# Trace of a batched matrix product: A's columns for five rows of B, transposed by VectorE in 32x32 blocks and copied from quadrant to quadrant, in place of TensorE transposes

## The chip, the cores and the metric

The kernel runs on one core of one Trainium2 chip. A core has a matrix engine (TensorE, PE in the profile), a vector engine (VectorE, DVE), a scalar engine (ScalarE, ACT), GpSimd (POOL) and a synchronisation engine (SyncE, SP), one on-chip memory of 128 partitions (SBUF), an accumulator memory (PSUM), and 16 DMA engines. The metric is the device time of one execution in microseconds (us); less is better.

## The reference

```python
def setup_inputs():
    B, N = 8, 2176
    return {"a": np.random.randn(B, N, N).astype(np.float32),
            "b": np.random.randn(B, N, N).astype(np.float32)}

def reference(a, b):
    prod = np.matmul(a, b)
    traces = np.diagonal(prod, axis1=1, axis2=2).sum(axis=-1)
    return traces.astype(np.float32)
```

Only the diagonal of each product is summed, so each of the eight results is the sum over i and j of a[i, j] * b[j, i]: every element of A and of B is used once, A transposed against B. A and B are read once each, 2 x 8 x 2176 x 2176 x 4 bytes, 303 MB.

## The kernel before, in words

A matrix is 17 blocks of 128 rows ("rows" below always means such blocks of 128). `load` brings rows from DRAM to SBUF through `fetch`, a DMA issued by POOL that casts float32 to bf16 on the way. `fetch` issues every load in one fixed order: `in_order` ties each issue to the one before. In a group of m rows, partition p holds the m consecutive matrix rows m*p to m*p + m - 1, so that each partition reads one long run of DRAM.

For a batch the loads are A's first five rows (into pool `middle`, one buffer), A's other twelve (`stage`, two buffers of twelve rows; two groups of six in one DMA), then B's five (`middle` again) and B's twelve (`stage`). The lists are `a_loads = b_loads = [(1, 5), (2, 6)]`. Batch 0 starts with one row of A that SP loads as float32 and ScalarE and VectorE cast (`load_first`), then four, then twelve; the last batch loads A's twelve before its five, and B in small pieces.

`transpose_group` turns one group of A's rows into the tile `at` ([128, 17, 2176] bf16, one buffer), whose layout matches B's. Because B's groups interleave rows too (`even = [5, 6, 6]`), the columns of A that belong to one of B's rows lie bm apart, with bm the rows of B's group. For B's groups of an even number of rows, pairs of neighbouring bf16 columns are read as one float32 word and transposed together by TensorE (L151); for the group of five, `singles`, they are transposed one at a time as bf16 (L175). The results go to PSUM tiles `ps` (three buffers of pool `psum`, tag `aT`), and `evacuate` copies them into `at`: every fourth copy by VectorE (L121), the others by ScalarE (L123).

When A's 17 rows of a batch stand in `at`, `on_dve` issues `multiply_reduce` on VectorE (L128) for B's five rows and then for B's twelve: each multiplies `at` by the rows of B, writes the product over `at` and sums it into one column of `sums`. `tc.issue_after` puts these behind the batch's last VectorE copy. The last batch gives part of B to TensorE (L287), and its B groups are `fine = [4, 4, 4, 2, 1, 1, 1]`, which have no group of five.

The waits around the change: POOL's load of B's five rows needs `middle` free, so it waits for the last transpose that reads A's five rows. POOL's load of the next batch's five rows of A needs `middle` free again, so it waits for the multiply-reduce of B's five rows, which in turn needs the whole of `at`, so all copies of A's twelve rows. Behind it in POOL's order stands the load of the next batch's twelve rows. The next batch's copies into `at` wait for the multiply-reduces that read it. Tile, the framework, places the waits; each engine runs its instructions in order.

Of the kernel before, what the change touches and what calls it, by code (L numbers as in the profile page):

```python
# [20 lines left out]
def kernel(  # L21
# [6 lines left out]
    nc = tc.nc  # L28
    P = 128
    BATCH, N, N2 = a.shape  # L30
    assert N == N2 and N % P == 0
    NT = N // P
    MOST, MID = 12, 5

    bf16 = mybir.dt.bfloat16
    f32 = mybir.dt.float32
# [21 lines left out]
    at_pool = ctx.enter_context(tc.tile_pool(name="at_pool", bufs=1))  # L58
    stage = ctx.enter_context(tc.tile_pool(name="stage", bufs=2))
    middle = ctx.enter_context(tc.tile_pool(name="middle", bufs=1))  # L60
    single = ctx.enter_context(tc.tile_pool(name="single", bufs=1))
    psum_pool = ctx.enter_context(tc.tile_pool(name="psum", bufs=3, space=bass.MemoryType.PSUM))
    psum_small = ctx.enter_context(tc.tile_pool(name="psum_small", bufs=1, space=bass.MemoryType.PSUM))

# [22 lines left out]
    def load_first(src, start):  # L87

        words = stage.tile([P, MOST, N], bf16, tag="stage")
        plain = words.bitcast(f32).rearrange("p r k -> p (r k)")[:, :N]  # L90
        half = N // 2
        t = single.tile([P, 1, N], bf16, tag="single")
        nc.sync.dma_start(out=plain, in_=src[start:start + P, :])
        nc.scalar.copy(out=t[:, 0, :half], in_=plain[:, :half])  # L94
        nc.vector.tensor_copy(out=t[:, 0, half:], in_=plain[:, half:])  # L95
        return t
# [18 lines left out]
    evacs = 0  # L115
    last_copy = None

    def evacuate(dst, src):
        nonlocal evacs, last_copy
        if evacs % 4 == 3:  # L120
            last_copy = nc.vector.tensor_copy(out=dst, in_=src)  # L121
        else:
            nc.scalar.copy(out=dst, in_=src)  # L123
        evacs += 1

    def multiply_reduce(x, y, acc, out=None):

        nc.vector.tensor_tensor_reduce(  # L128
            out=x if out is None else out, in0=x, in1=y, scale=1.0, scalar=0.0,
            op0=MUL, op1=ADD, accum_out=acc,  # L130
        )

    def transpose_group(at, a_t, start, m, b_groups):

        words = a_t.bitcast(f32)
        dst = at[:, :, start:start + P * m].rearrange("q v (p r) -> q v p r", r=m)
        pairs, singles = [], []
        for b_start, bm in b_groups:
            v = b_start // P
            if bm % 2 == 0:  # L140
                for t in range(bm // 2):
                    pairs.append((v + 2 * t, b_start // 2 + t, bm // 2))
            else:
                singles += [(v + r, b_start + r, bm) for r in range(bm)]

        for at0 in range(0, len(pairs), 8 // m):
            some = pairs[at0:at0 + 8 // m]
            ps = psum_pool.tile([P, 8, P], f32, tag="aT")
            for n, (v, c0, step) in enumerate(some):
                for r in range(m):  # L150
                    nc.tensor.transpose(  # L151
                        ps[:, n * m + r, :],
                        words[:, r, c0:c0 + step * (P - 1) + 1:step],
                        tiles[f32],
                    )
            if m == 1:
                v0 = some[0][0]
                evacuate(
                    dst[:, v0:v0 + 2 * len(some), :, 0].rearrange("q (n s) p -> q n s p", s=2),
                    ps.bitcast(bf16).rearrange("q n (p s) -> q n s p", s=2)[:, 0:len(some), :, :],  # L160
                )
                continue
            for n, (v, _, _) in enumerate(some):
                evacuate(
                    dst[:, v:v + 2, :, :],
                    ps[:, n * m:(n + 1) * m, :].bitcast(bf16).rearrange("q r (p s) -> q s p r", s=2),
                )
        for at0 in range(0, len(singles), 16 // m):
            some = singles[at0:at0 + 16 // m]
            ps = psum_pool.tile([P, 8, P], f32, tag="aT")  # L170
            ps16 = ps.bitcast(bf16).rearrange("q a b -> q (a b)")[:, 0:len(some) * m * P]
            ps16 = ps16.rearrange("q (n r p) -> q n r p", r=m, p=P)
            for n, (v, c0, step) in enumerate(some):
                for r in range(m):
                    last_transpose = nc.tensor.transpose(  # L175
                        ps16[:, n, r, :],
                        a_t[:, r, c0:c0 + step * (P - 1) + 1:step],
                        tiles[bf16],
                    )
            v0 = some[0][0]  # L180
            evacuate(dst[:, v0:v0 + len(some), :, :], ps16.rearrange("q n r p -> q n p r"))
        return last_transpose

    pe_work = []
# [13 lines left out]
    for bi in range(BATCH):  # L198
        last = bi == BATCH - 1
        b_groups = row_groups(P, fine if last else even)  # L200


        at = at_pool.tile([P, NT, N], bf16, tag="at")
        at_row = 0
        for g, m in last_loads if last else a_loads if bi else first_loads:
            start = at_row * P
            at_row += g * m
            if not tiles:
                a_t = load_first(a[bi], start)
                ahead = load(a[bi], start + P * m, *first_loads[1])  # L210
                with tc.issue_after(loaded[-1].ins):
                    constants()
            elif ahead is not None:
                a_t, ahead = ahead, None
            else:
                a_t = load(a[bi], start, g, m)
            for s in range(g):
                last_transpose = transpose_group(
                    at, a_t[:, s * m:(s + 1) * m, :], start + s * m * P, m, b_groups
                )  # L220


        copies_end = last_copy
        acc = tiles["late"] if last else tiles["sums"][:, bi * per_batch:(bi + 1) * per_batch]
        cols = 0

        def on_dve(v0, rows):

            nonlocal cols
            m = rows.shape[1]  # L230
            with tc.issue_after(copies_end.ins):
                multiply_reduce(
                    at[:, v0:v0 + m, :].rearrange("q v x -> q (v x)"),
                    rows.rearrange("q v x -> q (v x)"),
                    acc[:, cols:cols + 1],
                )
            cols += 1

        if not last:
            at_row = 0  # L240
            for g, m in b_loads:
                on_dve(at_row, load(b[bi], at_row * P, g, m))
                at_row += g * m
            continue

        used = MOST
        for start, m in b_groups:
            v0 = start // P
            if start < N - P:

                if used + m > MOST:
                    shared = stage.tile([P, MOST, N], bf16, tag="stage")
                    used = 0
                b_t = fetch(shared[:, used:used + m, :], b[bi], start, 1, m)
                used += m
                if v0 == SHARED_ROW:
                    row = b_t[:, 0, :]
                    multiply_on_pe(at, row, v0, 0, HALF)
                    keep_pe_busy(at, v0)
                    late.append((at[:, v0, HALF:], row[:, HALF:]))  # L260
                    continue
                mine = [s for s in range(m) if v0 + s not in PE_ROWS]
                if mine:
                    on_dve(v0 + mine[0], b_t[:, mine[0]:mine[-1] + 1, :])
                for s in range(m):
                    if s not in mine:
                        multiply_on_pe(at, b_t[:, s, :], v0 + s, 0, N)
                        keep_pe_busy(at, v0 + s)
                continue
            row = shared[:, used, :]  # L270
            for lo, mid, hi in LAST_PIECES:
                with in_order():
                    loaded.append(nc.gpsimd.dma_start(  # L273
                        out=row[:, lo:hi], in_=b[bi, start:start + P, lo:hi]
                    ))
                multiply_on_pe(at, row, v0, mid, hi)
                if mid > lo:
                    late.append((at[:, v0, lo:mid], row[:, lo:mid]))
# [5 lines left out]
    for n, (x, y) in enumerate(pe_work):  # L284
        real = y.shape[-1] == P
        with tc.issue_after(before.ins):
            before = nc.tensor.matmul(  # L287
                trace_ps if real else unread[:, 0:4, :], x, y,
                start=(n == 0 or not real), stop=(n == len(pe_work) - 1 or not real),
# [7 lines left out]
        out=result[:1, 0:done],  # L297
        in_=total[:, 0:early].rearrange("o (b n) -> o b n", n=per_batch),
        axis=mybir.AxisListType.X,
    )  # L300
    for x, y in late:
# [8 lines left out]
        out=result[:1, done:BATCH], in_=total[:, early:early + cols], axis=mybir.AxisListType.X  # L310
    )
    nc.sync.dma_start(
        out=out.rearrange("(a b) -> a b", a=1),
# [32 lines left out]
```

## Time and profile before

| what | value |
|---|---|
| median of 3 runs | 708.83 us (708.82 to 708.97) |
| span of the profiled execution | 707.1 us, 1.7 us below the median of the runs; no other time is given for that execution |
| PE, busy | 200.8 us (28%) |
| DVE, busy | 386.8 us (55%), 98 instructions |
| ACT, busy | 202.9 us (29%), 160 instructions |
| POOL, busy | 24.7 us (3%) |
| bytes written by DMA, and read from HBM | 152.31 MB, 303.04 MB |
| L151, PE, float32 transposes | 833, 147.1 us |
| L175, PE, bf16 transposes | 646, 45.8 us |
| L123, ACT, copies PSUM to `at` | 158, 200.5 us |
| L121, DVE, copies PSUM to `at` | 52, 83.4 us |
| L128, DVE, multiply-reduce of 12 and of 5 rows | 7 of 27.36 us, 7 of 11.49 us |

The span is the time between the first and the last recorded instruction. An engine's busy share is over the whole span; engines overlap, so the shares don't add to 100%. L123 is a line of the kernel's source; where a helper issues an instruction, the line is the helper's. Sizes such as 128x1536 are partitions by elements per partition.

### The profile page before, as it was taken

What the parts mean: (1) busy time and instruction counts of PE and PEld (TensorE: products, weight loads), DVE (VectorE), ACT (ScalarE), POOL (GpSimd) and SP (SyncE); (2) the same over time, 40 slices, a digit from 0 to 9 for tenths busy, and PEclk for the clock granted to TensorE, in tenths of its full rate; (3) what the DMA queues carried; (4) which work ended last, traced back from release to release, by engine and by line L of the source; (5) the groups of instructions that cost most, each with busy time, mean ns of one, the idle gap of its engine ahead of it and who ended that gap; (6) DMA issues with size and microseconds to landing.
All of it is one profiled execution on the core that took longest, in us unless ns stands there. A gap on an engine that the chain in (4) does not pass through costs nothing.

```text
span 707.1 us, 3653 instructions
## 1 busy us (share of the span) xinstructions
PE 200.8 (28%) x1569; PEld 179.8 (25%) x1569; DVE 386.8 (55%) x98; ACT 202.9 (29%) x160; POOL 24.7 (3%) x47
## 2 busy tenths in 40 slices
PE   2235003450134501344012440134301353003806
PEld 1234002440123401243012430124301343003703
DVE  0105488154881539616397163961629627395497
ACT  2327002470024700346004350044500445002910
POOL 1000000000000000000000000000000000000100
PEclk9759555695557955678556785567755677555957
DMA  9999999999999999999999999999999999999997
GB/s 236 213 217 212 225 206 214 216 224 214 224 215 213 223 213 214 216 223 218 215 217 216 215 222 213 216 223 211 221 216 216 222 214 217 216 220 213 217 211 151
DMA packets 7698, 152.31 MB, mean 215 GB/s; under 512 B 642, under 2 KB 898, under 8 KB 1282
## 3 DMA queue, kind: packets, MB, share of 16 engines
q0 software_dynamic: 7536, 150.96, 99.6%
q1 hardware_dynamic: 146, 1.11, 0.4%
q8 instruction: 12, 0.20, 0.1%
q14 instruction: 4, 0.03, 0.0%
HBM read 303.04 MB, written 0.00 MB: 429 GB/s over the span
## 4 chain that ended last, share of the span: by engine, by line
DVE 33%; another core or an unknown queue 27%; ACT 13%; PE 12%; DMA 11%; issue 3%; POOL 0%; ACTq 0%; DVEq 0%; POOLq 0%
DVE at L128 33%; ACT at L123 13%; PE ps L151 9%; DMA t<-in_a_dram 6%; DMA shared<-in_b_dram 5%; PE ps L175 2%; DVE at L121 0%; POOL shared L75 0%; PE trace_ps L287 0%; POOL shared L273 0%; POOL identity masks.py:199 0%; POOL identity masks.py:197 0%; ACTq L123 0%; DVE diagonal L128 0%
## 5 line engine op out<-in xcount | busy, mean ns | idle before, releaser
L123 ACT COPY at<-ps 128x1536 bf16<-128x1536 bf16 (+5 forms) x158 | 200.5, 1359 | 467.2 <-DVE sums L128 308.6
L128 DVE CUSTOM_DVE_ANT_0 at<-at,t 128x10880 bf16<-128x10880 bf16 (+1 forms) x14 | 272.0, 19426 | 96.3 <-DMA t<-in_b_dram 86.6
L151 PE MATMUL ps<-identity,t 128*128 128x128 f32 x833 | 147.1, 344 | 471.6 <-DMA t<-in_a_dram 378.6
L151 PEld LDWEIGHTS ps<-identity,t 128*128 128x128 f32 x833 | 131.3, 209 | 484.6 <-issue 380.3
L121 DVE COPY at<-ps 128x1536 bf16<-128x1536 bf16 (+3 forms) x52 | 83.4, 1604 | 205.8 <-PE ps L151 152.5
L175 PE MATMUL ps<-identity,t 128*128 128x128 bf16 x646 | 45.8, 227 | 11.0 <-ACT at L123 8.6
L175 PEld LDWEIGHTS <-t 128*128 128x128 bf16 x646 | 43.1, 119 | 14.7 <-issue 14.2
L128 DVE CUSTOM_DVE_ANT_0 at<-at,shared 128x8704 bf16<-128x8704 bf16 (+4 forms) x6 | 29.9, 5001 | 1.8 <-DMA shared<-in_b_dram 1.7
L75 POOL DMA_DIRECT2D t<-in_a_dram x16 | 10.1, 637 | 294.1 <-DVE sums L128 267.4
L75 POOL DMA_DIRECT2D t<-in_b_dram x14 | 8.7, 628 | 290.8 <-PE ps L175 290.5
L287 PEld LDWEIGHTS <-at 128*128 128x128 bf16 x86 | 6.8, 112 | 24.7 <-issue 23.9
L287 PE MATMUL trace_ps<-shared,at 128*128 128x128 bf16 x71 | 5.8, 241 | 21.0 <-DMA shared<-in_b_dram 20.9
L75 POOL DMA_DIRECT2D shared<-in_b_dram x6 | 3.2, 541 | 59.3 <-DVE sums L128 38.9
L287 PE MATMUL unread<-at 128*128 128x512 bf16 x15 | 5.2, 496 | 0.0
L296 DVE TENSOR_REDUCE result<-total 1x7 f32<-1x14 f32 x1 | 0.2, 159 | 7.8 <-PE total L295 7.8
L95 DVE CAST t<-words 128x1088 bf16<-128x1088 f32 x1 | 0.7, 727 | 4.9 <-DMA words<-in_a_dram 4.9
L94 ACT CAST t<-words 128x1088 bf16<-128x1088 f32 x1 | 1.1, 1099 | 3.7 <-DMA words<-in_a_dram 3.7
L273 POOL DMA_DIRECT2D shared<-in_b_dram x3 | 1.6, 552 | 1.9 <-DMA shared<-in_b_dram 1.9
L94 ACT ACT_TABLE_LOAD x1 | 1.3, 1283 | 0.7 <-PEq L330 0.7
L128 DVE DVE_READ_ACCUMULATOR2_ANT sums<- 128x1 f32 x14 | 1.2, 83 | 0.0
L128 DVE CUSTOM_DVE_ANT_0 diagonal<-identity,trace_ps 128x128 bf16<-128x128 f32 x1 | 0.3, 289 | 0.6 <-PE trace_ps L287 0.6
L128 DVE DVE_READ_ACCUMULATOR2_ANT late<- 128x1 f32 x7 | 0.6, 83 | 0.0
(12 smaller groups left out, 2.1 us busy)
## 6 DMA issues: line engine op xcount, KB each, us to landing
t<-in_a_dram POOLq DMA_DIRECT2D x8, 6528.0 KB, 55.1
t<-in_b_dram POOLq DMA_DIRECT2D x7, 6528.0 KB, 52.8
t<-in_b_dram POOLq DMA_DIRECT2D x7, 2720.0 KB, 22.1
t<-in_a_dram POOLq DMA_DIRECT2D x7, 2720.0 KB, 24.8
shared<-in_b_dram POOLq DMA_DIRECT2D x3, 2176.0 KB, 36.0
t<-in_a_dram POOLq DMA_DIRECT2D x1, 2176.0 KB, 14.7
words<-in_a_dram SPq DMA_DIRECT2D x1, 1088.0 KB, 5.0
shared<-in_b_dram POOLq DMA_DIRECT2D x1, 1088.0 KB, 30.5
```

The source lines that it names most:

```text
L75: issued = nc.gpsimd.dma_start(out=t.rearrange("p (g r) k -> p g (r k)", g=g), in_=rows)
L94: nc.scalar.copy(out=t[:, 0, :half], in_=plain[:, :half])
L95: nc.vector.tensor_copy(out=t[:, 0, half:], in_=plain[:, half:])
L121: last_copy = nc.vector.tensor_copy(out=dst, in_=src)
L123: nc.scalar.copy(out=dst, in_=src)
L128: nc.vector.tensor_tensor_reduce(out=x if out is None else out, in0=x, in1=y, scale=1.0, scalar=0.0, op0=MUL, op1=ADD, accum_out=acc,)
L151: nc.tensor.transpose(ps[:, n * m + r, :], words[:, r, c0:c0 + step * (P - 1) + 1:step], tiles[f32],)
L175: last_transpose = nc.tensor.transpose(ps16[:, n, r, :], a_t[:, r, c0:c0 + step * (P - 1) + 1:step], tiles[bf16],)
L273: loaded.append(nc.gpsimd.dma_start(out=row[:, lo:hi], in_=b[bi, start:start + P, lo:hi]))
L287: before = nc.tensor.matmul(trace_ps if real else unread[:, 0:4, :], x, y, start=(n == 0 or not real), stop=(n == len(pe_work) - 1 or not ...
L296: nc.vector.reduce_sum(out=result[:1, 0:done], in_=total[:, 0:early].rearrange("o (b n) -> o b n", n=per_batch), axis=mybir.AxisListType.X,)
```

## The change

For every group of A's rows in the first seven batches, the columns that belong to B's group of five rows no longer go through TensorE and PSUM. The new function `turn_group` does two steps. First VectorE transposes 32x32 blocks: one instruction for each of the five rows of B, 128 partitions by m x 128 elements (m rows of A in the group), reading A's columns five apart, writing into a new tile `turned` (pool `turned`, one buffer). Each block of 32 columns is then right within its 32 partitions (a quadrant), but the blocks stand in the quadrant that they came from. Then 16 copies, one for each source quadrant and target block, carry 32 partitions by 5 x 32m elements from one quadrant to another, into `at`. Every third copy is ScalarE's, the others VectorE's. So a group of six rows has five transposes of 128x768 and 16 copies of 32x960; a group of five rows, 128x640 and 32x800.

In those batches `evacuate` gives all PSUM copies to ScalarE (`on_act`). The last batch, without a group of five, still uses TensorE for all and gives VectorE every fourth copy. In the order of instructions, ScalarE does the evacuations of a group and then its copies from `turned`; the next group's transposes wait until `turned` has been read. Over the kernel there are 110 VectorE transposes, 235 quadrant copies on VectorE and 117 on ScalarE; 51 of the 646 bf16 transposes on TensorE stay.

Two smaller edits: `load_first` casts into the last row of its own staging buffer, and pool `single` goes; and each multiply-reduce on VectorE is issued after the one before it, where all of a batch's were issued after the batch's last copy.

The diff, cut to its core:

```diff
-    MOST, MID = 12, 5
+    MOST, MID, MID_UP = 12, 5, 6
+    Q, QUADS = 32, 4
...
-    single = ctx.enter_context(tc.tile_pool(name="single", bufs=1))
+    turn_pool = ctx.enter_context(tc.tile_pool(name="turned", bufs=1))
...
-        t = single.tile([P, 1, N], bf16, tag="single")
+        t = words[:, MOST - 1:MOST, :]
...
-    def evacuate(dst, src):
+    def evacuate(dst, src, on_act):
         nonlocal evacs, last_copy
-        if evacs % 4 == 3:
+        if evacs % 4 == 3 and not on_act:
...
+    turns = 0
+
+    def turn_group(at, a_t, start, m, b_start, bm):
+
+        nonlocal turns, last_copy
+        v = b_start // P
+        turned = turn_pool.tile([P, bm, QUADS, Q * MID_UP], bf16, tag="turned")
+        turned = turned[:, :, :, 0:Q * m]
+        for r in range(bm):
+            nc.vector.transpose(
+                out=turned[:, r].rearrange("p c (y s) -> p s c y", s=m),
+                in_=a_t[:, :, b_start + r:b_start + r + bm * (P - 1) + 1:bm].rearrange(
+                    "p s (c y) -> p s c y", y=Q),
+            )
+        for source in range(QUADS):
+            lo = start + source * Q * m
+            for c in range(QUADS):
+                dst = at[c * Q:(c + 1) * Q, v:v + bm, lo:lo + Q * m]
+                src = turned[source * Q:(source + 1) * Q, :, c, :]
+                if turns % 3 == 2:
+                    nc.scalar.copy(out=dst, in_=src)
+                else:
+                    last_copy = nc.vector.tensor_copy(out=dst, in_=src)
+                turns += 1
...
-            else:
-                singles += [(v + r, b_start + r, bm) for r in range(bm)]
+            elif bm > 1:
+                turned.append((b_start, bm))
+            else:
+                singles.append((v, b_start, bm))
...
+        for b_start, bm in turned:
+            turn_group(at, a_t, start, m, b_start, bm)
...
-        copies_end = last_copy
+        in_front = last_copy
...
-            with tc.issue_after(copies_end.ins):
-                multiply_reduce(
+            with tc.issue_after(in_front.ins):
+                in_front = multiply_reduce(
```

More of the change, by code (lines that the diff above doesn't have):

```diff
@@ L126, in multiply_reduce @@
     def multiply_reduce(x, y, acc, out=None):
-        nc.vector.tensor_tensor_reduce(
+        return nc.vector.tensor_tensor_reduce(
             out=x if out is None else out, in0=x, in1=y, scale=1.0, scalar=0.0,
@@ L136, in transpose_group @@
         dst = at[:, :, start:start + P * m].rearrange("q v (p r) -> q v p r", r=m)
-        pairs, singles = [], []
+        pairs, singles, turned = [], [], []
         for b_start, bm in b_groups:
@@ L150, in transpose_group @@
                 for r in range(m):
-                    nc.tensor.transpose(
+                    last_transpose = nc.tensor.transpose(
                         ps[:, n * m + r, :],
@@ L160, in transpose_group @@
                     ps.bitcast(bf16).rearrange("q n (p s) -> q n s p", s=2)[:, 0:len(some), :, :],
+                    turned,
                 )
@@ L166, in transpose_group @@
                     ps[:, n * m:(n + 1) * m, :].bitcast(bf16).rearrange("q r (p s) -> q s p r", s=2),
+                    turned,
                 )
+        for b_start, bm in turned:
+            turn_group(at, a_t, start, m, b_start, bm)
         for at0 in range(0, len(singles), 16 // m):
@@ L180, in transpose_group @@
             v0 = some[0][0]
-            evacuate(dst[:, v0:v0 + len(some), :, :], ps16.rearrange("q n r p -> q n p r"))
+            evacuate(
+                dst[:, v0:v0 + len(some), :, :], ps16.rearrange("q n r p -> q n p r"), turned,
+            )
         return last_transpose
@@ L227, in on_dve @@
         def on_dve(v0, rows):
-            nonlocal cols
+            nonlocal cols, in_front
             m = rows.shape[1]
-            with tc.issue_after(copies_end.ins):
-                multiply_reduce(
+            with tc.issue_after(in_front.ins):
+                in_front = multiply_reduce(
                     at[:, v0:v0 + m, :].rearrange("q v x -> q (v x)"),
```

## The prediction, made before the changed kernel had run

> **What bounds the kernel now.** I read the page first: its slices and its DMA queues.
>
> ```profile
> DMA  9999999999999999999999999999999999999997
> GB/s 236 213 217 212 225 206 214 216 224 214 224 215 213 223 213 214 216 223 218 215 217 216 215 222 213 216 223 211 221 216 216 222 214 217 216 220 213 217 211 151
> ...
> q0 software_dynamic: 7536, 150.96, 99.6%
> ...
> HBM read 303.04 MB, written 0.00 MB: 429 GB/s over the span
> ```
>
> The DMA row is at nine tenths or more in all slices but the last: the 16 DMA engines never pause, and nearly every byte is on POOL's queue. 303 MB of HBM reads in a span of 707.1 us is the whole time; VectorE (55% busy), ScalarE (29%) and TensorE (28%) have room. So an edit of engine work matters only if it keeps the DMA queue from being fed. The times: the profiled execution spans 707.1 us, the median of the runs is 708.83 us, 1.7 us more for what lies around the span. I predict on the runs' scale: 708.83 plus what the span grows by.
>
> Next I ask where the queue is closest to running dry, with the timeline of one batch (columns: start us, us taken, engine, line, operation, count, idle time before and its releaser).
>
> ```profile
> 126.43 1.25 POOL L75 DMA_DIRECT2D t<-in_b_dram  x2 [46.41 <-PE ps L175]
> 135.22 5.29 PEld L151 LDWEIGHTS ps<-identity,t 128*128 128x128 f32 x30 [9.25 <-issue]
> 135.26 5.46 PE L151 MATMUL ps<-identity,t 128*128 128x128 f32 x30 [9.13 <-DMA t<-in_a_dram]
> 136.87 8.86 ACT L123 COPY at<-ps 128x1536 bf16<-128x1536 bf16 x7 [9.64 <-PE ps L151]
> ...
> 146.08 8.86 ACT L123 COPY at<-ps 128x1536 bf16<-128x1536 bf16 x7 [0.35 <-PE ps L151]
> ...
> 151.32 1.76 DVE L121 COPY at<-ps 128x1536 bf16<-128x1536 bf16 x1 [2.05 <-PE ps L175]
> ...
> 154.97 11.49 DVE L128 CUSTOM_DVE_ANT_0 at<-at,t 128x10880 bf16<-128x10880 bf16 x1 [1.89 <-ACT at L123]
> ...
> 166.77 1.25 POOL L75 DMA_DIRECT2D t<-in_a_dram  x2 [39.09 <-DVE sums L128]
> 178.77 27.36 DVE L128 CUSTOM_DVE_ANT_0 at<-at,t 128x26112 bf16<-128x26112 bf16 x1 [12.30 <-DMA t<-in_b_dram]
> ```
>
> At 135.26 A's twelve rows have landed and TensorE starts on them. Copies to `at` end on ScalarE and VectorE at 154.97: I call these 19.7 us the conversion. Then VectorE's multiply-reduce of B's five rows (11.49 us) frees the buffer `middle`, and only then, at 166.77, POOL issues the next batch's first five rows of A. What keeps the DMA engines busy meanwhile is B's twelve rows, issued at 126.43, which land at 178.77. In the trace's packet records their bytes give way to those five rows at 177.2 us on the first of the 16 engines and at 178.4 on the last. So POOL is 177.2 - 166.77 = 10.4 us early. This window comes once a batch, at six transitions (from batch 6 to 7 twelve rows of A lead the order, and those don't wait for the multiply). The earlier issue of B, at 126.43, stands 7 us before the last bytes of A's twelve rows (133.5 in the packet records) and follows the conversion of five rows, which the change shortens on TensorE.
>
> How much of the 10.4 us is lead, from POOL's start to the first packet? No row shows it for a dry queue. SP's first DMA has its first packet 1.0 us after its start; POOL's first one, started at 1.23, has its first packet at 5.0, but right behind SP's packets, so 3.7 us is an upper end. I take the 0.55 us of POOL's shortest DMA instruction plus SP's 1.0: 1.6 us. The conversion may grow by 10.4 - 1.6 = 8.8 us before the first engine idles, and by 10.0 before the last does, which alone sets when a load has landed. Per us beyond, six transitions cost 6 us.
>
> **The change, part by part.** Prices come from these rows (busy us, mean ns of one):
>
> ```profile
> L123 ACT COPY at<-ps 128x1536 bf16<-128x1536 bf16 x97 | 132.4, 1460 | 145.7 <-PE ps L151 145.7
> ...
> L121 DVE COPY at<-ps 128x1536 bf16<-128x1536 bf16 x32 | 56.3, 1758 | 152.7 <-PE ps L151 132.3 <-PE ps L175 13.3 <-ACT at L123 7.1
> ...
> L75 POOL DMA_DIRECT2D t<-in_a_dram x16 | 10.1, 637 | 294.1 <-DVE sums L128 267.4 <-PE ps L175 25.9 <-POOLq L330 0.8
> ...
> L121 DVE COPY at<-ps 128x768 bf16<-128x768 bf16 x4 | 3.8, 958 | 7.7 <-PE ps L175 7.7
> ...
> L94 ACT CAST t<-words 128x1088 bf16<-128x1088 f32 x1 | 1.1, 1099 | 3.7 <-DMA words<-in_a_dram 3.7
> ...
> L95 DVE CAST t<-words 128x1088 bf16<-128x1088 f32 x1 | 0.7, 727 | 4.9 <-DMA words<-in_a_dram 4.9
> ```
>
> *Removed.* TensorE loses 595 of its 646 bf16 transposes (17 rows of A by 5 rows of B, in seven batches), VectorE nearly all its PSUM evacuations there, and both engines the evacuations of those five rows. In a twelve-row conversion that was 18 evacuations (twelve of 1536, four of 1536 and two of 768 for the five rows of B), 14 of them on ScalarE. None lies on what sets the time, so the gain is nothing.
>
> *Evacuations now all on ScalarE.* Two groups of six, 1536 elements each. One takes 1460 ns alone; seven in a row (six of 1536, one of 768) took 8.86 us, and six of 1536 spaced by 1.34 us elsewhere in the trace (8.15 us less the last one's 1.46, by 5). So 6 x 1.34 = 8.0 us a group.
>
> *Transposes on VectorE.* Five per group, 128x768 bf16. No 32x32 transpose is in the trace. The nearest row has the same 768 elements, a copy at 958 ns; I take 0.96 us, 4.8 us a group. Bounds: 0.80 (768 elements at the pace between the 768 and 1536 rows, no fixed part) and 1.92 (two passes).
>
> *Quadrant copies.* Sixteen per group, 32x960 bf16 from SBUF to SBUF; of a twelve-row conversion's 32, VectorE has 21 and ScalarE 11 (six, then five). For ScalarE the only SBUF-to-SBUF row is L94: 1099 ns for 1088 elements, so about 0.99 us for 960, and queued ones start some 0.1 us earlier, as the evacuations do: 0.89; bounds 0.84 (the evacuations' 1.34 us for 1536, per element) and 1.10 (L94 whole). For VectorE, L95 took 727 ns for 1088 SBUF elements, which leaves 0.16 us fixed (as in 768 against 1536) and two elements per cycle: 0.66 for 960. Its PSUM rows run at half that pace: 1758 ns for 1536 gives 1.16 us for 960. I take 0.66, the row with the same memory at both ends; 1.16 is the upper end and 0.50, L95's pace with nothing fixed, the lower.
>
> The Trainium skill, "VectorE: DVE Perf Modes", section "The perf-mode tier table", gives a bf16 SBUF copy four elements per cycle (693 ns for 2048) and any PSUM source two at most; the PSUM row here shows one. By the page a copy would take about 0.41 us, an estimate, and the sum below would not move, since ScalarE ends last anyway. The same page's "Rules for kernel authors" speaks against the change: it sends 128x128 transposes to TensorE and keeps VectorE's for 32x32 blocks, whose price for 128 columns it gives as 311 ns; by that a 768-column one is an estimated 0.98 us, and the sum again stays.
>
> *Sum for twelve rows, on the timeline's clock.* ScalarE: first evacuation at 136.87, six end by 144.9; six copies (the transposes that they wait for ended at 135.3 + 4.8 = 140.1) to 150.2. VectorE's ten copies of that group end at 140.1 + 6.6 = 146.7. Pool `turned` has one buffer, so the second group's transposes wait for ScalarE's last copy: 150.3 to 155.1, and eleven copies to 162.4. ScalarE: six evacuations, 150.2 to 158.2 (TensorE has filled three PSUM tiles ahead), five copies to 162.7. Conversion: 162.7 - 135.3 = 27.4, growth 7.7 us. That eats most of the 8.8, but leaves 1.1 us on the first DMA engine and 2.3 on the last.
>
> *The other waits that are added.* VectorE's multiply-reduce of B's five rows is queued behind the transposes and copies, and POOL behind that: counted. POOL's issue of B now waits also for VectorE's five transposes of five-row A (640 elements, about 4.2 us from 118.8, so 123.0) beside TensorE, which without its 25 transposes ends near 123.7: earlier than 126.4. That five-row conversion ends on ScalarE at 119.0 + 6 x 1.12 + 5 x 0.76 = 129.5, before 135.26. ScalarE's first copies of batch 0 wait for A's second load, with over 20 us before the next one lands. In the last batch no group has five rows; only which evacuations VectorE takes shifts, worth well under 1 us before reduces that already wait for their loads. The first load's bf16 copy moves into its own staging buffer, read long before that is loaded again.
>
> **Rivals.**
>
> *Overrun by the serial chain.* One mechanism: the order evacuate, copy, evacuate, copy on ScalarE, tied by the single `turned` buffer, comes out longer than the window. With 1.10 us copies the conversion is 11 x 0.21 = 2.3 us longer (growth 10.0); with 1.92 us transposes and 0.66 us copies VectorE becomes last (144.9, 151.5, 161.1, 168.4: growth 13.4). It decides from a growth of 8.8 to 10.0 us on; with lead 1.6 these two give 708.8 + 6 x 0 to 1.2 = 709 to 716 and 6 x 3.4 to 4.6 = 729 to 736; a lead of 3.7 adds up to 12.6. For it: the margin is 1 to 2 us and three prices come from other operations. Against: each must be wrong upwards. 0.28, mostly near 711 to 720.
>
> *VectorE copies at PSUM pace.* With 1.16 us copies VectorE ends last: 140.1 + 11.6 = 151.7, transposes to 156.5, copies to 169.3; growth 14.3, beyond the window by 4.3 to 5.5, times six: 735 to 742. Against: L95 reads SBUF at twice that pace. 0.12.
>
> *Faster.* If freeing TensorE and VectorE let loads start earlier, or ended the tail sooner. The DMA rows leave no gap to close; only the last 3 us behind the last bytes could shrink, by less than 1.5. 0.04.
>
> **How the numbers follow.** Window kept, 0.56: 708.83 + 0, with packet jitter and the shifted evacuations of the tail within 1 us: 708 to 710. Overrun 0.28, PSUM pace 0.12, faster 0.04. The range from 708.0 to 719.0 holds the first case, over two thirds of the second, and part of the fourth, about 0.8. One measurement of this kernel tells about 0.2%, 1.4 us, from no change. Same: the first case, 0.56; slower: 0.40; faster: 0.04.
>
> **What would show it.** Right: the DMA row stays at nines, the multiply-reduce of B's five rows starts about 27 us after twelve rows landed, POOL's issue of A's five rows comes some 2 to 3 us before B's twelve rows land, VectorE's busy time rises by some 160 us (110 transposes, 235 copies, less 45 evacuations) and ScalarE's by about 80 with no effect on the span. Wrong: gaps in DMA and GB/s rows once a batch, with VectorE waiting on loads after a POOL issue that came later than B's landing; the row to read then is the mean of the 32x960 copies and the 128x768 transposes.

## The result: 762.1 us, 7.5% slower

The changed kernel's median is 762.07 us (760.86 to 762.90, 5 runs), beside 708.83 us for the kernel before (708.82 to 709.09, 5 runs): ratio 1.0747, 95% interval 1.0734 to 1.0760. The forecast of 708.9, in a range of 708.0 to 719.0, missed it by 53 us.

The page of the changed kernel, its busy times, its slices and its DMA queue:

```profile
PE 177.2 (23%) x972; PEld 152.3 (20%) x974; DVE 657.6 (86%) x398; ACT 296.2 (39%) x265; POOL 24.8 (3%) x47
...
DMA  9999799997899987999969999699995999999997
GB/s 220 220 216 217 154 191 218 211 223 154 169 219 220 212 178 147 220 221 211 199 132 221 219 215 212 126 218 209 222 220 112 215 220 216 214 220 217 214 218 152
...
q0 software_dynamic: 7536, 150.96, 93.3%
```

The DMA row, all nines before, falls to between seven and five tenths at six places, and the GB/s row to between 112 and 154 in its lowest slices there; POOL's queue works for 93.3% of 16 engines' span, before 99.6%. The bytes are the same. VectorE rose from 386.8 to 657.6 us.

The timeline of the same stretch of a batch that the prediction worked through (start us, us taken, engine, line, operation, count, idle time before and its releaser):

```profile
143.14 13.21 DVE L143 STREAM_TRANSPOSE turned<-t 128x768 bf16<-128x768 bf16 x5 [6.01 <-DMA t<-in_a_dram]
...
156.38 5.99 ACT L154 COPY at<-turned 32x960 bf16<-32x960 bf16 x6 [3.17 <-DVE turned L143]
156.38 4.62 DVE L156 COPY at<-turned 32x960 bf16<-32x960 bf16 x10
...
162.41 13.06 DVE L143 STREAM_TRANSPOSE turned<-t 128x768 bf16<-128x768 bf16 x5 [1.41 <-ACT at L154]
...
175.50 5.08 DVE L156 COPY at<-turned 32x960 bf16<-32x960 bf16 x11
180.71 11.49 DVE L129 CUSTOM_DVE_ANT_0 at<-at,t 128x10880 bf16<-128x10880 bf16 x1
...
192.13 27.35 DVE L129 CUSTOM_DVE_ANT_0 at<-at,t 128x26112 bf16<-128x26112 bf16 x1
192.51 1.25 POOL L76 DMA_DIRECT2D t<-in_a_dram  x2 [58.19 <-DVE sums L129]
```

Twelve rows of A land at 143.14 and the multiply-reduce of B's five rows starts at 180.71: the conversion takes 37.6 us, where 27.4 was summed and 19.7 stood before. VectorE carries it nearly alone: five transposes in 13.21 us, ten copies, a wait of 1.41 us for ScalarE's copies, five transposes in 13.06, eleven copies. The multiply-reduce of B's twelve rows then follows at 192.13 without any wait for its load, whose last packet ended at 186.4 by the packet records. POOL issues A's next five rows only at 192.51, when the DMA engines have been dry for 6 us. Their next packet comes at 193.8.

The transposes in the groups of instructions, shapes kept apart (busy us, mean ns of one | idle before):

```profile
L143 DVE STREAM_TRANSPOSE turned<-t 128x768 bf16<-128x768 bf16 x70 | 184.0, 2864 | 69.4 <-DMA t<-in_a_dram 59.5 <-ACT at L154 9.8
...
L143 DVE STREAM_TRANSPOSE turned<-t 128x640 bf16<-128x640 bf16 x30 | 54.7, 2013 | 0.0
...
L143 DVE STREAM_TRANSPOSE turned<-t 128x512 bf16<-128x512 bf16 x5 | 5.9, 1327 | 5.8 <-DMA t<-in_a_dram 5.8
```

A 128x768 transpose takes 2.86 us in the mean; in a row the next one starts before the one in front has ended, so five take 13.21 us, 2.64 each. Per element the three shapes give (1327 - 160)/512 = 2.3 ns with four rows of A, (2013 - 160)/640 = 2.9 with five, (2864 - 160)/768 = 3.5 with six, with 160 ns taken as the fixed part: it rises with m, the step between neighbours of the output.

### The profile page after: what moved, and what is told of

Read it like the earlier page. It is cut to its first block, busy times and chain, and to the rows that moved or that the text cites. A ratio compares the mean times of both kernels' runs of the same rounds, so it can differ in the third digit from the quotient of the medians.

```text
span 760.3 us, 2832 instructions
## 1 busy us (share of the span) xinstructions
PE 177.2 (23%) x972; PEld 152.3 (20%) x974; DVE 657.6 (86%) x398; ACT 296.2 (39%) x265; POOL 24.8 (3%) x47
## 3 DMA queue, kind: packets, MB, share of 16 engines
q0 software_dynamic: 7536, 150.96, 93.3%
## 5 line engine op out<-in xcount | busy, mean ns | idle before, releaser
L124 ACT COPY at<-ps 128x1536 bf16<-128x1536 bf16 (+2 forms) x146 | 186.8, 1384 | 341.1 <-DVE sums L129 234.7
L143 DVE STREAM_TRANSPOSE turned<-t 128x768 bf16<-128x768 bf16 (+2 forms) x105 | 244.5, 2548 | 75.2 <-DMA t<-in_a_dram 65.3
L179 PE MATMUL ps<-identity,t 128*128 128x128 f32 x827 | 161.4, 370 | 551.8 <-DMA t<-in_a_dram 409.1
L179 PEld LDWEIGHTS ps<-identity,t 128*128 128x128 f32 x827 | 140.7, 212 | 572.2 <-issue 405.8
L154 ACT COPY at<-turned 32x960 bf16<-32x960 bf16 (+3 forms) x117 | 107.0, 915 | 85.9 <-DVE turned L143 84.7
L156 DVE COPY at<-turned 32x960 bf16<-32x960 bf16 (+3 forms) x235 | 98.8, 420 | 3.6
L122 DVE COPY at<-ps 128x1536 bf16<-128x1536 bf16 (+2 forms) x7 | 11.0, 1568 | 12.6 <-PE ps L179 6.9
L207 PE MATMUL ps<-identity,t 128*128 128x128 bf16 x51 | 3.5, 219 | 0.6 <-ACT at L124 0.5
L207 PEld LDWEIGHTS <-t 128*128 128x128 bf16 x51 | 3.1, 97 | 1.1 <-issue 0.8
```

Of the source, the lines that this page charges most:

```text
L143: nc.vector.transpose(out=turned[:, r].rearrange("p c (y s) -> p s c y", s=m), in_=a_t[:, :, b_start + r:b_start + r + bm * (P - 1) + 1:bm ...
L179: last_transpose = nc.tensor.transpose(ps[:, n * m + r, :], words[:, r, c0:c0 + step * (P - 1) + 1:step], tiles[f32],)
L207: last_transpose = nc.tensor.transpose(ps16[:, n, r, :], a_t[:, r, c0:c0 + step * (P - 1) + 1:step], tiles[bf16],)
```

## The experiments

### What a transpose costs by itself

Why 2.86 us and not 0.96? This kernel only runs single instructions, four of each on a line of its own, with TensorE and DMA idle beside them. Its core, with line numbers and remarks added; L67 to L70 are spread(5) to spread(2) from five, L71 to L73 output steps of 2, 4 and 8 from near(6), and L77 to L82 copies of 32x960, three on VectorE and then three on ScalarE: plain, with an output step of 6, with an input step of 32:

```diff
+    def five(m):   # input columns five apart, as in the change
+        return src[:, 0:m, 1:1 + 5 * 127 + 1:5].rearrange("p s (c y) -> p s c y", y=32)
+    def near(m):   # input columns side by side
+        return src[:, 0:m, 0:128].rearrange("p s (c y) -> p s c y", y=32)
+    def spread(m): # output step m, as in the change
+        return turned[:, 0, 0:128 * m].rearrange("p (c y s) -> p s c y", c=4, s=m)
+    def dense(m):
+        return turned[:, 0, 0:128 * m].rearrange("p (s c y) -> p s c y", c=4, s=m)
...
+    for _ in range(4): nc.vector.transpose(out=dense(6), in_=near(6))    # L63
+    for _ in range(4): nc.vector.transpose(out=dense(6), in_=five(6))    # L64
+    for _ in range(4): nc.vector.transpose(out=spread(6), in_=near(6))   # L65
+    for _ in range(4): nc.vector.transpose(out=spread(6), in_=five(6))   # L66
...
```

Expected: 

> Not the trace of a product: only transposes and copies, four of each kind one after the other, no other engine at work beside them, so the time of the run means nothing and only the durations per line count. Question: why a 128x768 transpose took 2.86 us where 0.96 was predicted. Theory 1, scattered writes: the cost follows the step of the output (m elements between neighbours). Then a transpose with dense output takes about 0.95 us whether its input columns lie side by side or five apart, and with m = 2, 3, 4, 5, 6 it climbs in proportion to m, to about 2.8 us at 6, whatever the input. Theory 2, scattered reads: the step of five on the input costs; then dense input gives 0.95 us with either output, and a step of five gives 2.8 us with either. Theory 3, company: PE, ScalarE or DMA traffic slowed them in the kernel; then all kinds take about 0.95 us here. Copies of 32x960: plain ones 0.45 us on VectorE and 0.99 on ScalarE as in the changed kernel; with an output step of 6 (which would move the interleaving from the transpose to the copy) theory 1 says nothing for certain: 1.2 us if a copy doesn't suffer from scattered writes, 3 us or more if it does.

Measured, the groups by line:

```profile
L66 DVE STREAM_TRANSPOSE turned<-src 128x768 bf16<-128x768 bf16 x4 | 11.7, 2933 | 0.0
L65 DVE STREAM_TRANSPOSE turned<-src 128x768 bf16<-128x768 bf16 x4 | 11.7, 2923 | 0.0
L78 DVE COPY dst<-turned 32x960 bf16<-32x960 bf16 x4 | 8.3, 2067 | 0.1
...
L72 DVE STREAM_TRANSPOSE big<-src 128x768 bf16<-128x768 bf16 x4 | 7.3, 1834 | 0.0
...
L71 DVE STREAM_TRANSPOSE big<-src 128x768 bf16<-128x768 bf16 x4 | 4.0, 1002 | 7.1 <-DMA src<-in_a_dram 7.1
L64 DVE STREAM_TRANSPOSE turned<-src 128x768 bf16<-128x768 bf16 x4 | 4.0, 991 | 0.0
...
L63 DVE STREAM_TRANSPOSE turned<-src 128x768 bf16<-128x768 bf16 x4 | 3.7, 927 | 0.0
...
L77 DVE COPY dst<-turned 32x960 bf16<-32x960 bf16 x4 | 1.8, 450 | 0.1
```

Input five apart or side by side hardly matters (991 ns in L64, 927 in L63). The output does: with step 6 the same transposes take 2933 and 2923 ns (L66, L65); with step 4 they take 1834 (L72), with step 2 1002 (L71). The company of other engines has no share: 2.93 us here alone, 2.86 in the kernel. (In the trace L71 to L73 run in turn with L63 to L65, not one line after the other.) Theory 1 holds, with one correction: step 2 is nearly free, and it is from step 3 on that the time climbs, by 0.54 to 0.60 ns per element and unit of step ((2933 - 160)/768/6 = 0.60, (1834 - 160)/768/4 = 0.54). Copies suffer as well: the same 32x960 copy takes 450 ns plain on VectorE (L77) and 2067 with an output step of 6 (L78); ScalarE's goes from 988 (L80) to 3386 (L81). With an input step of 32 and a dense output they take 1130 and 1788 (L79, L82).

### Is it the loop, or VectorE's total work?

Two kernels cut VectorE's work at different places of the changed kernel: `keep` is the number of B's rows that the multiply-reduce covers.

```diff
+            keep = 2 if m == 5 and not last else m      # half_b5
+            keep = 6 if m == 12 and not last else m     # half_b12
...
-                    at[:, v0:v0 + m, :].rearrange("q v x -> q (v x)"),
-                    rows.rearrange("q v x -> q (v x)"),
+                    at[:, v0:v0 + keep, :].rearrange("q v x -> q (v x)"),
+                    rows[:, 0:keep, :].rearrange("q v x -> q (v x)"),
```

Expected of the first: 

> The changed kernel, but the multiply-reduce of B's five rows covers two of the five in the first seven batches (three rows' products are left out). Theory 1, a serial loop: twelve rows of A land, conversion, multiply-reduce of five rows, POOL's issue, five rows, twelve rows; the DMA engines idle about 8 us at six transitions because this loop is too long. The multiply falls from 11.49 to an estimated 4.69 us, so each of six transitions is 6.8 us shorter: 762.1 - 41 = 721 us. Rival, VectorE as a whole is the bound (86% busy): seven times 6.8 us less work, 762.1 - 48 = 714 us; the two are told apart by the next run.

Expected of the second: 

> The changed kernel, but the multiply-reduce of B's twelve rows covers six of them in the first seven batches (the others' products are left out). VectorE loses 7 x 13.6 = 95 us of work. Theory 1, the serial loop: this work stands after POOL's issue and outside the loop, so the time stays at 762 us within 2. Rival, VectorE as a whole: the time falls to the 709 us of the kernel before, where DMA is the bound.

Measured, two runs each: 720.59 us with the five-row multiply cut, 761.68 with the twelve-row one cut. The timelines, first the one, then the other:

```profile
174.89 4.69 DVE L129 CUSTOM_DVE_ANT_0 at<-at,t 128x4352 bf16<-128x4352 bf16 x1
...
179.89 1.25 POOL L76 DMA_DIRECT2D t<-in_a_dram  x2 [50.30 <-DVE sums L129]
```

```profile
192.15 13.75 DVE L129 CUSTOM_DVE_ANT_0 at<-at,t 128x13056 bf16<-128x13056 bf16 x1
192.53 1.25 POOL L76 DMA_DIRECT2D t<-in_a_dram  x2 [69.35 <-DVE sums L129]
```

In front of POOL's issue, a multiply-reduce of 4.69 us in place of 11.49 gave 41.5 us back, 6 x 6.9. Behind that issue, one of 13.75 in place of 27.35 us took VectorE from 657.6 to 563.2 us busy and gave 0.4 us. So the loop through POOL's issue sets the time, not VectorE's share of 86%.

### Parts of the change alone

`only_five` turns only groups of fewer than six rows of A; `second_only` turns those and the second group of six, with all evacuations on ScalarE.

```diff
-            elif bm > 1:
+            elif bm > 1 and m < MID_UP:          # only_five
+            elif bm > 1 and not on_pe:           # second_only: on_pe for the first group of six
                 turned.append((b_start, bm))
             else:
-                singles.append((v, b_start, bm))
+                singles += [(v + r, b_start + r, bm) for r in range(bm)]
```

Expected of `only_five`: 

> The change done only for A's groups of five rows (and batch 0's four and one); groups of six use TensorE for B's five rows as in the kernel before. Theory 1, the serial loop: the twelve-row conversion is as short as before (about 20 us), so no transition runs dry: 708.8 us within 0.5, though VectorE keeps some 90 us of added transposes and copies (30 transposes of 2.0 us, 66 copies of 0.4). Rival, VectorE's total work: a good part of the loss stays, about 725 us.

Expected of `second_only`: 

> The change done in the five-row groups and in the second of the two groups of six; the first of them goes through TensorE, with all its evacuations on ScalarE. The transposes stay at 2.7 us. Theory 1, the loop: VectorE's five transposes start as the rows land and end 13.2 us later, its copies at 18.5 us, while ScalarE needs 1.6 + 11.5 + 8.0 + 5.0 = 26 us; growth 6.5 us plus 1.3 of lead is inside the 10.4: 708.8 us within 0.6. Rival, every slow transpose costs: half of the loss stays, 735 us.

Measured: `only_five` 709.09 us, ratio 1.0002 (0.9993 to 1.0012); `second_only` 709.25 us, ratio 1.0005 (0.9995 to 1.0014). Both are within noise of the kernel before, though VectorE runs 462 us in `only_five` against 387. In `second_only` five transposes, 2.65 us apart, stand in every twelve-row conversion:

```profile
135.21 13.27 DVE L143 STREAM_TRANSPOSE turned<-t 128x768 bf16<-128x768 bf16 x5 [2.84 <-DMA t<-in_a_dram]
...
161.72 11.49 DVE L129 CUSTOM_DVE_ANT_0 at<-at,t 128x10880 bf16<-128x10880 bf16 x1 [8.12 <-ACT at L154]
...
178.76 27.36 DVE L129 CUSTOM_DVE_ANT_0 at<-at,t 128x26112 bf16<-128x26112 bf16 x1 [5.54 <-DMA t<-in_b_dram]
```

The conversion lasts 161.72 - 135.21 = 26.5 us, ScalarE ends it, and the multiply of B's twelve rows waits 5.54 us for its load: the window still holds. One slow group fits beside ScalarE's evacuations; two in a row on VectorE do not. The single buffer `turned` has little part in that: in the changed kernel VectorE waited 1.41 us for it, and its transposes and copies alone take 36.0 of the 37.6 us. No run has a second buffer.

### Transposes at the price that was predicted

`dense_out` leaves everything as in the change, but the transposes write densely.

```diff
-                out=turned[:, r].rearrange("p c (y s) -> p s c y", s=m),
+                out=flat[:, r].rearrange("p (s c y) -> p s c y", s=m, y=Q),
```

Expected: 

> The changed kernel, but the transposes write their 768 elements densely and the copies from quadrant to quadrant stay plain, so the columns of B's five rows stand in a wrong order in the first seven batches. Everything else, the order and the waits too, is the changed kernel's. Theory 1, scattered writes are the only term that was mis-sized: a 128x768 transpose falls to about 1.0 us, the twelve-row conversion to 29 us (ScalarE: six evacuations of 1.34 us, six copies of 1.0, six evacuations, five copies; growth 9.2 us), which with 1.3 us of lead just fits the window of 10.4 us: 708.8 to 710 us. Rival, the serial order itself (one turned buffer, evacuations all on ScalarE) costs more than the sum said: 715 us or more.

Measured: 719.27 us, ratio 1.0149 (1.0128 to 1.0169), so most of the 53 us was the transposes' writes, but not all. Its timeline:

```profile
136.69 4.85 DVE L144 STREAM_TRANSPOSE turned<-t 128x768 bf16<-128x768 bf16 x5 [9.38 <-DMA t<-in_a_dram]
...
166.00 11.49 DVE L129 CUSTOM_DVE_ANT_0 at<-at,t 128x10880 bf16<-128x10880 bf16 x1 [3.27 <-ACT at L155]
...
177.80 1.25 POOL L76 DMA_DIRECT2D t<-in_a_dram  x2 [52.47 <-DVE sums L129]
```

and its DMA queue:

```profile
q0 software_dynamic: 7536, 150.96, 98.8%
```

Transposes 0.97 us apart, ScalarE last, conversion 166.00 - 136.69 = 29.3 us, growth 9.6. The conversion is as long as expected, but the time is longer: 708.8 to 710 was forecast, and 10.3 us were lost, a time that the rival had named, though not by its mechanism: the serial order took 29.3 us where 29 was expected. So it is the window that was taken too wide. Growth and a lead of 1.3 make 10.9 us, 0.5 more than the 10.4 to the first engine's end, which for six transitions is only 3 us. The packet records tell the whole of it. The queue's packets fill 708.9 of the span's 717.5 us (98.8%) on the mean engine, before 704.4 of 707.1: it was without packets for 5.9 us more, and its packets took 4.5 us longer, together the 10.4 us by which the span grew. Nearly all of the longer packets (4.2 of the 4.5 us) are those of the five-row loads: after a dry queue the first packet of an engine takes 1.9 to 2.2 us on average where 1.62 is the rule. Why it does is not shown.

### The interleaving moved into the copies

```diff
-                out=turned[:, r].rearrange("p c (y s) -> p s c y", s=m),
+                out=turned[:, r].rearrange("p s (c y) -> p s c y", y=Q),
...
-                src = turned[source * Q:(source + 1) * Q, :, c, :]
+                dst = dst.rearrange("q v (y s) -> q v y s", s=m)
+                src = turned[source * Q:(source + 1) * Q, :, :, c * Q:(c + 1) * Q]
+                src = src.rearrange("q v s y -> q v y s")
```

Expected: 

> Dense transposes, and the copies from quadrant to quadrant do the interleaving: they read with a step of 128 elements and write densely. Priced alone, such a copy took 1.13 us on VectorE and 1.79 on ScalarE, against 0.45 and 0.99 for plain ones. Theory 1 (the loop): second group's end on VectorE at about 143 + 5.0 + 6 x 1.79 behind the evacuations, then 5.0 + 12.4: the conversion is again 37 to 38 us and the time 755 to 765 us: the scatter has only moved. Rival, only the transposes matter: 709 us.

Measured: 777.76 us (ratio 1.0970, 1.0946 to 1.0994): worse than the change, and above the 755 to 765 expected.

```profile
L158 DVE COPY at<-turned 32x960 bf16<-32x960 bf16 x147 | 192.1, 1307 | 2.3
```

The scatter had only moved, and VectorE's copies came dearer in the kernel, 1307 ns, than alone, 1130, so the conversion lasted 40.4 us, not 37 to 38. The two are not the same copy: here the input step is 128 elements, as the expectation says, but the single instruction L79 read with a step of 32. Whether the step or the company of other engines costs the 177 ns, no run tells.

### A version with cheap writes

For groups of 6 and 4 rows of A the transposes put pairs of A's rows side by side (output step 2), and the copies move float32 words, which are such pairs.

```diff
+                nc.vector.transpose(
+                    out=store[:, r, 0:P * m].rearrange("p (h x t) -> p h t x", h=m // 2, t=2),
+                    in_=cols.rearrange("p (h t) x -> p h t x", t=2),
+                )
...
+                    dst = at.bitcast(f32)[c * Q:(c + 1) * Q, v:v + bm, lo // 2:lo // 2 + Q * h]
+                    dst = dst.rearrange("q v (y h) -> q v y h", h=h)
+                    src = store.bitcast(f32)[source * Q:(source + 1) * Q, :, 0:P * h]
+                    src = src.rearrange("q v (h x) -> q v x h", h=h)[:, :, c * Q:(c + 1) * Q, :]
```

Expected: 

> A whole version of the change with cheaper writes: for groups of 6 and 4 rows of A the transposes write with a step of two elements (pairs of A's rows side by side, priced alone at 1.00 us for 128x768), and the copies from quadrant to quadrant move 480 float32 words in place of 960 bf16, reading with a step of 128 words. Groups of five rows stay as in the changed kernel. Theory 1: transposes 1.0 us, VectorE copies 0.4 to 0.7 us, ScalarE copies 0.6 to 1.2; conversion 25 to 29 us, growth 5 to 9: 708.8 to 710 us, as before the change and not below, since DMA is then the bound again. Rival, a copy of scattered words costs as much per byte as one of bf16: 740 us or more.

Measured: 708.15 us, ratio 0.9987 (0.9978 to 0.9997). The groups that count:

```profile
L169 DVE COPY at<-store 32x480 f32<-32x480 f32 x147 | 70.0, 476 | 2.3
L145 DVE STREAM_TRANSPOSE store<-t 128x768 bf16<-128x768 bf16 x70 | 67.7, 1041 | 72.2 <-DMA t<-in_a_dram 40.1 <-ACT at L167 32.1
```

Transposes take 1.04 us, VectorE's copies 0.48, and ScalarE's, not shown, 0.74; the conversion is 26.2 to 26.5 us and the DMA row is nines again in all slices but the last, as before. It was measured a second time.

Expected: 

> The paired version once more, with more rounds, since its first 10 runs lay 0.13% below the kernel before (interval 0.02 to 0.22%). Theory 1: DMA is the bound in both, so it stands within 0.2% of the kernel before: 707.5 to 709.5 us. Rival: less work on TensorE and PSUM is worth something: 1 us or more below again, outside the interval.

Measured: 708.16 us beside 709.04, ratio 0.9988 (0.9979 to 0.9997). It undoes the loss and stands 0.12% under the kernel before, less than the 0.2% that counts here. Where that 0.9 us lies is not settled: neither kernel shows a gap in its DMA row, and the queue's packets fill the same 704.4 us in both.

### Which writes are dear

A last list of single instructions, all 128x384, output steps of 1 to 8 elements. L80 to L83 are float32 transposes with steps 1 to 4; L84 to L88 bf16 transposes with steps 1, 2, 3, 4, 6; L89 to L93 VectorE's bf16 copies from PSUM with steps 1, 2, 4, 6, 8; L94 to L97 ScalarE's with 1, 2, 4, 6.

```diff
+    for _ in range(4): nc.vector.transpose(out=wf(2, 384), in_=sf(384))      # L81, float32, step 2
+    for _ in range(4): nc.vector.transpose(out=wb(6, 384), in_=sb(384))      # L88, bf16, step 6
+    for _ in range(4): nc.vector.tensor_copy(out=wb(6, 384), in_=pb(384))    # L92
+    for _ in range(4): nc.scalar.copy(out=wb(6, 384), in_=pb(384))           # L97
```

Expected: 

> Again only single instructions, four of each, no product: 128x384 transposes of bf16 and float32 with output steps of 1 to 6 elements, and copies from PSUM to SBUF (1 to 8). Theory 1a, the distance between outputs in bytes sets the cost: bf16 at step 2 (4 bytes) and float32 at step 1 cost the same, about 0.55 us; float32 at step 2 (8 bytes) as much as bf16 at step 4, about 1.0 us, at step 3 (12 bytes) as bf16 at 6, about 1.5. Theory 1b, the count of elements skipped sets it: float32 at step 2 stays near 0.55 us. Copies from PSUM at one element per cycle: if the write side alone is the cause, they too slow down from step 3 or 4 on; if it belongs to transposes and to fast copies, all steps take about 0.55 us.

Measured:

```profile
L88 DVE STREAM_TRANSPOSE big<-src 128x384 bf16<-128x384 bf16 x4 | 5.8, 1452 | 0.1
L92 DVE COPY big<-ps 128x384 bf16<-128x384 bf16 x4 | 5.7, 1432 | 0.1
L97 ACT COPY big<-ps 128x384 bf16<-128x384 bf16 x4 | 5.7, 1432 | 0.1
...
L87 DVE STREAM_TRANSPOSE big<-src 128x384 bf16<-128x384 bf16 x4 | 4.1, 1028 | 0.1
...
L83 DVE STREAM_TRANSPOSE big<-src 128x384 f32<-128x384 f32 x4 | 3.4, 853 | 0.1
...
L81 DVE STREAM_TRANSPOSE big<-src 128x384 f32<-128x384 f32 x4 | 2.3, 579 | 0.1
```

A bf16 write with step 6 takes 1452, 1432 and 1432 ns as a transpose, a VectorE copy from PSUM and a ScalarE copy from PSUM: the write sets the pace in all three. It does not do so everywhere: in the first list VectorE's copy from SBUF, 128x768 with the same step of 6, took 1441 ns (L74, not shown), half of the transpose's 2923 (L65). Float32 at step 2 is free (579 ns), so the distance in bytes alone is not the law (bf16 at step 4, also 8 bytes, takes 1028, L87). Theory 1a falls there, and 1b doesn't fit exactly either: float32 at step 4 takes 853 (L83). Which law holds stays open.

## Why the prediction was wrong

**The step that failed is the price of the transposes**, a term of the sum: 0.96 us each, bounds 0.80 and 1.92, taken from a copy of as many elements; measured 2.86 us for one and 2.64 in a row. With it fell the statement that ScalarE ends the conversion last: VectorE does, and ScalarE waits 4.95 us for it. `dense_out`, with transposes 0.97 us apart, gives 42.8 of the 53.2 us back. The row that it was taken from writes densely, and so does every copy in the trace of before; the transposes write with a step of six elements. The bound of "two passes" was no bound, because nothing in the trace had that write pattern. The diff showed it: `"p c (y s) -> p s c y"`.

**The mechanism was the one described.** With the measured prices, 2.64 a transpose, 0.46 a VectorE copy and 1.00 a ScalarE copy, its own sum gives 13.2 + 6 x 1.00 (ScalarE's six, which end after VectorE's ten) + 13.1 + 5.1 = 37.4 us, beside the 37.6 seen. With 2.64 alone and its other prices it would have given 40.3, a loss of 64 to 71 us: VectorE's copies were priced too high. Growth 17.9, lead 1.3, window 10.4: 8.8 us a transition, times six 53 us; measured 53.2. That this meets the number so closely is partly luck. By the packet records the engines stood dry for 7.8 to 8.9 us at each of the six transitions, 48.8 us in all in the mean of the 16, and the packets of the five-row loads took 4.5 us longer; the sum has too much of the first and nothing of the second. The rival "overrun by the serial chain" had this form, with transposes as one of its two ways, but at 1.92 us it reached only 729 to 736, and its chance of 0.28 was "mostly near 711 to 720".

**Smaller terms.** ScalarE's copies: 0.89 taken, 1.00 measured (six in 5.99 us); queued SBUF copies did not overlap as the evacuations do. VectorE's copies: 0.66 taken, 0.45 to 0.46 measured, so the rival "PSUM pace" fell. The Trainium skill, "VectorE: DVE Perf Modes", section "The perf-mode tier table", had an estimated 0.41 for them, nearer than the row. The same page's section "The three transpose paths", by which a dense transpose of 768 columns was an estimated 0.98 us, agrees with the 0.93 to 0.99 measured for a dense output (L63, L64). Lead: 1.6 taken, 1.3 measured (POOL at 192.51, first packet at 193.8). The window: that only the last engine's end counts, 11.6 us after POOL's issue, did not hold, as `dense_out` lost 10.3 us where growth and lead made 10.9; an engine that runs dry earlier loses time too, and its first packet is slow. So the time would have left the range, narrowly, even at the predicted price: 719.27 against 719.0. A small misreading did no harm: 133.5, called the last bytes of A's twelve rows, is the end on the first of the 16 engines; on the last it is 134.8.

**What was right.** Nothing was gained by freeing TensorE and PSUM. POOL's issue of B, the start and the tail stayed harmless: all the dry time lies at the six transitions. The price asked for under "what would show it" was the right row to read.

**What stays open.** Why the first packets after a dry queue are slow, what made the interleaving copies dearer in the kernel than alone, and the 0.9 us by which the paired version is ahead.

## What to carry to other kernels

Before a price is taken from a row with the same element count, compare the access patterns too, the output's first: a write of bf16 elements three or more apart cost about 0.55 ns per element and unit of step here, in VectorE's transposes, in both engines' copies from PSUM and in ScalarE's from SBUF (0.28 to 0.33 in VectorE's copies from SBUF). If a layout needs such a step, write pairs with step 2 and move them on as 32-bit words. Where DMA is the bound, find the loop that issues the next load and sum it against its window; a margin of 1 us is worth little while the sum rests on an operation that the trace doesn't show.

## What the runs showed of the hardware

- 128x768 bf16 transposes by VectorE: 927 ns dense, 1002 with output step 2, 1834 with 4, 2933 with 6, 3644 with 8; an input step of five adds 64 ns to the dense one (991 ns).
- Copies between quadrants, 32x960 bf16: 450 ns on VectorE, 0.30 ns per element beyond a fixed 160 ns; 988 on ScalarE.
- A bf16 copy from PSUM, 128x384, with dense input and output takes 358 ns on VectorE, 0.52 ns per element beyond the fixed 160 ns. The kernel's evacuations, whose inputs are strided, take 1.04 (1758 ns for 1536 elements). No run shows whether the stride is the cause.
- A DMA queue that has run dry: POOL's start to the first packet 1.3 us, and the first packets, of 21,760 bytes, take about 2.3 us in the changed kernel where 1.62 is the rule.
